# Squared-ReLU MLP on one core: another order of terms, block sums, conversions and the tail around the Down stages

## The chip, the cores and the metric

The kernel runs on one core of a Trainium2 chip. The metric is device time in microseconds (us), the median of three runs. The engines are TensorE (PE in the profile, its weight loads PEld), VectorE (DVE), ScalarE (ACT), GpSimd (POOL) and SyncE (SP), which issues most of the DMA transfers. Each engine executes its own instructions in order; semaphores order them between engines.

## The reference

A decoder trunk of two layers on 512 tokens of width 1024, in float32. Layer A mixes tokens by a short gated convolution, layer B by native sparse attention; both then add a squared-ReLU MLP. The change touches only the MLPs and the final norm:

```python
def rms_norm(x, g):
    xf = x.astype(jnp.float32)
    y = xf * lax.rsqrt(jnp.mean(xf * xf, axis=-1, keepdims=True) + EPS)
    return (y * g.astype(jnp.float32)).astype(x.dtype)

def squared_relu_mlp(h, w1, w2):
    return jnp.square(jax.nn.relu(h @ w1)) @ w2        # w1 1024 x 4096, w2 4096 x 1024
...
        x = x + squared_relu_mlp(rms_norm(x, norm_mlp[layer]), mlp_w1[layer], mlp_w2[layer])
...
    return rms_norm(x, final_norm)
```

## The kernel before

**Numbers.** Every matrix product runs in fp16: each float32 operand is split into a high half (hi) and the rest (lo), and three matmuls make a term: hi·hi, hi·lo and lo·hi. The residual stream `X` stays in SBUF, features on the partitions, as 8 tiles of 128 x 512 tokens. The RMS norm's factor per token is not put on the MLP's input but on the result of the first product.

**Weights.** They come in *pieces* in the order in which they are used. A piece is loaded by SP into one of three staging slots (`wst`, L157 for the MLP's second matrix), then split: ACT writes the hi half (L184, L195), DVE the lo half (L185, L196). `ahead()` (L215) converts until AHEAD2 = 3 pieces of the second matrix (AHEAD = 2 of others) lie in front of the one in use; when a piece's conversion is through, the load of a later one into its slot is issued.

**MLP.** Each layer's MLP is done in two halves of 2048 hidden features. For each half `mlp_up` runs 8 pairs of hidden tiles, 48 matmuls of 512 columns a pair on PE (`mm3`, L341 to L343). Then for each pair (`mlp_up`, L499 to L505): DVE multiplies relu by the row factor `rb` (`ml_t`), ACT squares (`ml_z`, L501), POOL makes four sums of 256 columns (`R_SUMS`, L503), ACT writes the hi half `rh` (L504) and DVE the lo half `rl` (L505). The factor `rb` is made once in a layer, in the first pair: a matmul sums the squares, `rstd_of` (L295) takes ACT's square root (L298) and refines its inverse in five small DVE steps (L300 to L305; the last, L305, writes `rs_r`), PE spreads the row over the partitions (L312), ACT scales it (L317).

`mlp_down` multiplies by the second matrix with seven products in place of eight, by Winograd's scheme for 2 x 2 blocks: the four blocks of the weights give seven operands by four sums on DVE (`W_SUMS`, L182, in place in the staging slot, before the split), the hidden side has its seven from `R_SUMS`. There are 4 pairs of output tiles; a pair takes 8 chunks of the hidden features, a chunk 7 products of 3 matmuls (L550 hi·hi, L551 weight hi by relu lo, L552 weight lo by relu hi), 256 columns each. Chunk c reads what `mlp_up` wrote in its pair c, so the last chunk reads the last `rl`. A piece holds two chunks of weights, so a pair takes four pieces. The seven products are summed over the chunks in PSUM halves: pairs 0 and 2 in two banks `a` and two `b`, pairs 1 and 3 in two `c`, a `d` and an `e`. 

`combine` puts the seven results together into `X`: an ACT copy of P1 (`dn_p`, L520), then DVE steps (L517 with a scalar, L527, L531, L533). It is a generator, `post`: one step of it is issued after each chunk of the next pair, with the conversions of `ahead()` in between.

**The tokens' form of the result.** In the last of the four Down stages, `mid_b` is called after chunk 5 of a pair: `token_major` (L1168) has PE transpose the pair before into tokens on the partitions, in banks `a` or `c`. ACT squares (L1162) and copies (L1177, to `xsh` and `xsl` under the program's tile names) and POOL multiplies by the gains (L1178). The last pair is done by `last_b` (L1205): its first half as chunks, then its seven products one after the other, each with its combine steps behind it; the last transposes (L1166); and `store` (L1187) for two token tiles at a time: the sum of squares, the inverse root, the scaling (ACT half of the columns, L1195; DVE the others, L1198 to L1202) and the store on SP's queue (L1203).

**What sets the order.** The program is written in one order, and a scheduler moves instructions on each engine; `tc.issue_after(ins)` adds one edge, so that what is issued in its scope stands behind `ins` on that engine.

Of the kernel before, what the change touches and what calls it, by code (L numbers as in the profile page):

```python
# [48 lines left out]
def body(ctx, tc, x, rel_bias, norm_mix, norm_mlp, mlp_w1, mlp_w2, a_w_in, a_conv_w, a_w_out,  # L49
         kv_norm, w_kv, cmp_pe_k, cmp_pe_v, phi_k_w1, phi_k_w2, phi_v_w1, phi_v_w2,  # L50
         b_w_qg, b_w_o, final_norm, ident_c, onehot_c, out):
    nc = tc.nc
# [118 lines left out]
    def convert_piece(step=1024):  # L171
# [7 lines left out]
        if shape is None:  # L179
            b = t.rearrange("p (k b n) -> p k b n", k=2, n=128)  # L180
            for e, o, x, y in W_SUMS:
                DVE.tensor_tensor(b[:, :, o], b[:, :, x], b[:, :, y], op=e)  # L182
# [110 lines left out]

    def rstd_of(ss):
# [10 lines left out]
        DVE.scalar_tensor_tensor(r, t, 1.5, r, op0=OP.add, op1=OP.mult)  # L305
# [201 lines left out]

    def combine(p, acc7, done):
# [11 lines left out]
        ACT.activation(p1, P1, AF.Copy, scale=sc)  # L520
# [17 lines left out]
    def mlp_down(rh, done, mid=None, last=None):  # L538

        post = iter(())  # L540
        for p in range(4):
# [3 lines left out]
            def product(i, c, w):  # L545
                a, b = PRODUCTS[i]
                wh, wl = (u[:, a - 1] for u in w)
                xh, xl = (u[:, c, b - 1] for u in rh)
                other = i % 2 == 1
                PE.matmul(acc7[i], wh, xh, start=c == 0 and not other, stop=False, skip_group_check=other)  # L550
                PE.matmul(acc7[i], wh, xl, start=False, stop=False, skip_group_check=other)  # L551
                PE.matmul(acc7[i], wl, xh, start=False, stop=c == 7, skip_group_check=other)  # L552
# [20 lines left out]
            post = combine(p, acc7, done)  # L573
        drain(post)
# [570 lines left out]
    with pool("hidden_b") as hp:  # L1145
# [22 lines left out]
        def token_major(p, h, tag):  # L1168
# [4 lines left out]
            for i in range(2):  # L1173
# [3 lines left out]
                ACT.activation(o, v, AF.Copy)  # L1177
                POOL.tensor_tensor(o, o, gains(p), op=OP.mult)  # L1178

        def mid_b(p):  # L1180
            if p:
                for h in range(2):
                    token_major(p - 1, h, "a" if p % 2 else "c")
# [4 lines left out]
        def store(h, late=None):  # L1188
            sst = work.tile([128, 2], F32, name="sst", bufs=2)
            DVE.tensor_reduce(sst, ssf[:, 2 * h:2 * h + 2], axis=mybir.AxisListType.X, op=OP.add)  # L1190
            r = rstd_of(sst)
            for i in range(2):
                t = 2 * h + i
                a, b = xt[t][:, 0:512], xt[t][:, 512:1024]
                ACT.activation(a, a, AF.Copy, scale=r[:, i:i + 1])  # L1195
                if late:
                    b = xt[t][:, 512:768]
                    DVE.scalar_tensor_tensor(xt[t][:, 768:896], late[i], r[:, i:i + 1], gains(3, 1),  # L1198
# [85 lines left out]
```

## Time and profile before

| | us |
|---|---|
| median of three runs | 1137.95 (1136.97 to 1138.77) |
| profiled execution | 1136.88 |
| its span | 1135.1 |
| busy: PE | 1095.8 (97%) |
| busy: DVE | 832.3 (73%) |
| busy: ACT | 568.5 (50%) |
| busy: POOL | 157.6 (14%) |

The profile is one execution; its time stands beside its span, which begins with the first instruction. In the rows below a line begins with the start in us and the duration, then the engine, the line of the kernel, the operation, the tile written and those read, and in brackets the idle time ahead of it on its engine with what ended it. Rows that begin with two numbers and a colon are stretches of the span: the length, then the busy time of PE (count), PEld, DVE, ACT, POOL and SP, the granted TensorE clock, the DMA share and GB/s. A row of several instructions has "xcount", and the duration from the first start to the last end or their sum.

Each layer has up, Down, up, Down. The four Down stages begin at 266.4, 424.4, 882.5 and 1040.7 in the span; between the second and the third lie the shared K/V side, the attention and the first up stage of layer B.

### The profile page before, as it was taken

The numbers are of one execution on the slowest core, as the hardware profiler recorded it, in microseconds if no ns is written. First come the engines' busy times: TensorE is split into PE (matmuls) and PEld (weight loads), VectorE is DVE, ScalarE is ACT, GpSimd is POOL, SyncE is SP. The second block draws the span as 40 slices with busy tenths as digits, with TensorE's granted clock in tenths as the row PEclk, the third lists the DMA queues.
The fourth block names the chain that finished last, engine by engine and source line by source line (L and its number), as shares of the span: only waits on it lengthen the run. The fifth ranks groups of instructions, "written<-read, shape, count | busy, mean of one in ns | idle before, by whom it ended". The sixth has DMA issues, their size and how long they took to land.

```text
span 1135.1 us, 20099 instructions
## 1 busy us (share of the span) xinstructions
PE 1095.8 (97%) x7959; PEld 694.1 (61%) x7959; DVE 832.3 (73%) x1498; ACT 568.5 (50%) x922; POOL 157.6 (14%) x198
## 2 busy tenths in 40 slices
PE   8999999999999999999999989899999999999985
PEld 4444444446884448865767666664444787445874
DVE  4755458765897556999589969896895598754795
ACT  4532235444433444556679777765544433343452
POOL 0000000422000221001002022220122100123020
PEclk9999999999999999999999999999999999999998
DMA  6433335333333333313334341112633333330221
GB/s 210 130 94 97 107 105 172 113 93 113 112 112 112 111 95 107 112 42 120 112 78 122 83 138 38 39 38 74 187 111 112 111 109 115 105 95 7 84 84 75
DMA packets 149378, 115.75 MB, mean 102 GB/s; under 512 B 8612, under 2 KB 146564, under 8 KB 149284
## 3 DMA queue, kind: packets, MB, share of 16 engines
q1 hardware_dynamic: 146736, 109.47, 31.8%
q10 hardware_dynamic: 2260, 4.40, 1.3%
q8 instruction: 62, 1.02, 0.4%
q0 software_dynamic: 288, 0.61, 0.2%
q14 instruction: 32, 0.26, 0.1%
HBM read 110.22 MB, written 2.14 MB: 99 GB/s over the span
## 4 chain that ended last, share of the span: by engine, by line
PE 50%; DVE 19%; ACT 11%; issue 7%; POOL 7%; DMA 5%; SPq 1%; DVEq 0%; ACTq 0%; POOLq 0%
POOL ml_z L503 6%; PE a L341 4%; PE a L342 4%; PE a L343 4%; DVE wlo L185 4%; DMA wst<-mlp_w_dram 3%; ACT rh L504 3%; PE c L343 3%; PE c L342 3%; PE c L341 3%; PE b L342 3%; PE b L341 3%; PE b L343 3%; DVE wlo L196 3%; DVE ml_t L499 2%
## 5 line engine op out<-in xcount | busy, mean ns | idle before, releaser
L195 ACT ACTIVATE whi<-wst 128x1024 f16<-128x1024 f32 (+4 forms) x171 | 142.4, 858 | 127.9 <-PE b L342 38.4
L196 DVE SCALAR_TENSOR_TENSOR wlo<-wst,whi 128x1024 f16<-128x1024 f32 (+4 forms) x171 | 169.9, 1001 | 40.2 <-ACT whi L195 39.9
L503 POOL TENSOR_TENSOR ml_z<-ml_z 128x256 f32<-128x256 f32 x128 | 99.9, 801 | 610.1 <-ACT ml_z L501 410.1
L184 ACT ACTIVATE whi<-wst 128x1792 f16<-128x1792 f32 x64 | 106.9, 1692 | 135.4 <-DVE wst L182 102.3
L341 PEld LDWEIGHTS <-whi 128*128 128x128 f16 x1024 | 100.4, 98 | 112.3 <-issue 5.5
L343 PEld LDWEIGHTS <-wlo 128*128 128x128 f16 x1024 | 100.2, 98 | 112.1 <-issue 0.4
L342 PEld LDWEIGHTS <-whi 128*128 128x128 f16 x1024 | 100.2, 98 | 107.6 <-issue 2.0
L505 DVE TENSOR_TENSOR rl<-ml_z,rh 128x1792 f16<-128x1792 f32 x32 | 64.8, 2026 | 135.9 <-ACT rh L504 135.7
L185 DVE SCALAR_TENSOR_TENSOR wlo<-wst,whi 128x1792 f16<-128x1792 f32 x64 | 128.8, 2019 | 3.0 <-ACT whi L184 2.9
L182 DVE TENSOR_TENSOR wst<-wst 128x256 f32<-128x256 f32 x256 | 108.9, 469 | 24.4 <-DMA wst<-mlp_w_dram 23.4
L504 ACT ACTIVATE rh<-ml_z 128x1792 f16<-128x1792 f32 x32 | 54.3, 1698 | 106.1 <-POOL ml_z L503 106.1
L551 PEld LDWEIGHTS <-whi 128*128 128x128 f16 x896 | 87.7, 98 | 16.2 <-issue 5.6
L552 PEld LDWEIGHTS <-wlo 128*128 128x128 f16 x896 | 87.6, 98 | 15.0 <-issue 4.2
L550 PEld LDWEIGHTS <-whi 128*128 128x128 f16 x896 | 87.7, 98 | 10.5
L343 PE MATMUL b<-xsh,wlo 128*128 128x512 f16 x208 | 78.8, 379 | 0.0
L342 PE MATMUL b<-xsl,whi 128*128 128x512 f16 x208 | 78.8, 379 | 0.0
L341 PE MATMUL b<-xsh,whi 128*128 128x512 f16 x208 | 78.7, 379 | 0.0
L501 ACT ACTIVATE ml_z<-ml_t 128x1024 f32<-128x1024 f32 x32 | 33.8, 1057 | 88.4 <-DVE ml_t L499 88.4
L963 ACT ACTIVATE at_p<-at_s,at_m 128x128 f32<-128x128 f32 (+3 forms) x128 | 71.0, 557 | 13.7 <-DVE at_m L961 12.6
L551 PE MATMUL a<-rl,whi 128*128 128x256 f16 x256 | 69.8, 273 | 3.7 <-DVE rl L505 3.7
L341 PE MATMUL c<-xsh,whi 128*128 128x512 f16 x192 | 72.8, 379 | 0.0
L342 PE MATMUL c<-xsl,whi 128*128 128x512 f16 x192 | 72.8, 379 | 0.0
(309 smaller groups left out, 2686.4 us busy)
## 6 DMA issues: line engine op xcount, KB each, us to landing
wst<-mlp_w_dram SPq DMA_DIRECT2D x256, 256.0 KB, 3.3
wst<-a_w_in_dram SPq DMA_DIRECT2D x18, 512.0 KB, 3.5
wst<-w_kv_dram SPq DMA_DIRECT2D x12, 512.0 KB, 3.5
T<-ext_d ACTq DMA_DIRECT2D x4, 1056.0 KB, 6.0
wst<-a_w_out_dram SPq DMA_DIRECT2D x8, 512.0 KB, 3.4
wst<-b_w_qg_dram SPq DMA_DIRECT2D x8, 512.0 KB, 3.5
wst<-b_w_o_dram SPq DMA_DIRECT2D x8, 512.0 KB, 3.3
wst<-a_w_in_dram SPq DMA_DIRECT2D x8, 384.0 KB, 5.5
```

The costliest lines, as they stand in the source:

```text
L182: DVE.tensor_tensor(b[:, :, o], b[:, :, x], b[:, :, y], op=e)
L184: ACT.activation(hi, b[:, :, 1:], AF.Copy, scale=sc)
L185: DVE.scalar_tensor_tensor(lo, b[:, :, 1:], sc, hi, op0=OP.mult, op1=OP.subtract)
L195: ACT.activation(hi[:, s:e], w, AF.Copy, scale=sc)
L196: DVE.scalar_tensor_tensor(lo[:, s:e], w, sc, hi[:, s:e], op0=OP.mult, op1=OP.subtract)
L341: PE.matmul(ps, w[0], xs[0], start=start, stop=False)
L342: PE.matmul(ps, w[0], xs[1], start=False, stop=False)
L343: PE.matmul(ps, w[1], xs[0], start=False, stop=stop)
L503: POOL.tensor_tensor(z[:, o], z[:, a], z[:, b], op=e)
L504: ACT.activation(rh[0][:, p], z[:, 1:8], AF.Copy)
L550: PE.matmul(acc7[i], wh, xh, start=c == 0 and not other, stop=False, skip_group_check=other)
L551: PE.matmul(acc7[i], wh, xl, start=False, stop=False, skip_group_check=other)
```

## The change

It has four parts.

1. *Order of terms.* In every product of `mlp_down` the weight's lo half is now taken second and relu's lo half third. In the first pair's last chunk all seven products take their first two terms first, and then all seven the third.
2. *Block sums.* `W_SUMS` of a piece are issued behind the last step of the inverse root that was built last (`root_op`). And `combine`'s first step (P6, P7) is issued as soon as it exists, ahead of the next pair's conversions.
3. *Conversions behind the copies.* In the first chunk of each later pair the conversions are issued behind the ACT copy `dn_p` of the pair before. In the last stage those of chunk 4 move to after chunk 5, behind the last ACT copy of the tokens.
4. *Tail.* The last pair's products run in the order P1, P6, P5, P7, P3, P2, P4. The first two token tiles are scaled by DVE alone, all columns, behind the sum of P4; for the other two ACT scales the lower half of the columns and stores it on its own queue, DVE the upper, stored on SP's.

```diff
@@ convert_piece
-            for e, o, x, y in W_SUMS:
-                DVE.tensor_tensor(b[:, :, o], b[:, :, x], b[:, :, y], op=e)
+            with tc.issue_after(root_op[0].ins):
+                for e, o, x, y in W_SUMS:
+                    DVE.tensor_tensor(b[:, :, o], b[:, :, x], b[:, :, y], op=e)
@@ rstd_of
-        DVE.scalar_tensor_tensor(r, t, 1.5, r, op0=OP.add, op1=OP.mult)
+        root_op[0] = DVE.scalar_tensor_tensor(r, t, 1.5, r, op0=OP.add, op1=OP.mult)
@@ combine
-        ACT.activation(p1, P1, AF.Copy, scale=sc)
+        copied[0] = ACT.activation(p1, P1, AF.Copy, scale=sc)
@@ mlp_down
-            def product(i, c, w):
+            def product(i, c, w, terms=(0, 1, 2)):
...
-                PE.matmul(acc7[i], wh, xh, start=c == 0 and not other, stop=False, skip_group_check=other)
-                PE.matmul(acc7[i], wh, xl, start=False, stop=False, skip_group_check=other)
-                PE.matmul(acc7[i], wl, xh, start=False, stop=c == 7, skip_group_check=other)
+                for n in terms:
+                    PE.matmul(acc7[i], wl if n == 1 else wh, xl if n == 2 else xh, stop=c == 7 and n == 2,
+                              start=c == 0 and n == 0 and not other, skip_group_check=other)
...
-                    for i in range(7):
-                        product(i, c + k, [u[:, k] for u in w])
-                    if c + k == 5 and mid:
-                        mid(p)
-                    if k == 0:
-                        drain(ahead())
-                    next(post, None)
+                    for terms in ((0, 1), (2,)) if p == 0 and c + k == 7 else ((0, 1, 2),):
+                        for i in range(7):
+                            product(i, c + k, [u[:, k] for u in w], terms)
+                    behind = None
+                    if c + k == 0 and p:
+                        behind = copied[0]
+                    if c + k == 5 and mid and p:
+                        behind = mid(p)
+                    if k == (1 if c == 4 and mid else 0):
+                        with tc.issue_after(behind.ins) if behind else nullcontext():
+                            drain(ahead())
+                    if c + k or not p:
+                        next(post, None)
...
             post = combine(p, acc7, done)
+            next(post)
@@ last_b
             product(2)
             stt(wv[:, 1], P6, p1)
             DVE.tensor_tensor(X1[:, n1], X1[:, n1], p1, op=OP.add)
+            product(4)
+            stt(both, P5[:, None, :].to_broadcast([128, 2, 256]), both)
             product(3)
             stt(wv[:, 0], P7, wv[:, 1])
             DVE.tensor_tensor(both, both, wv, op=OP.add)
-            product(4)
-            stt(both, P5[:, None, :].to_broadcast([128, 2, 256]), both)
...
-                DVE.tensor_tensor(xt[t][:, 768:1024], ps[:, 0:256], gains(3), op=OP.mult)
-            store(0)
+                early.append(ps[:, 0:256])
+            r = root(0)
...
-                DVE.tensor_tensor(xt[t][:, 896:1024], ps[:, 0:128], gains(3)[:, 128:256], op=OP.mult)
+                early.append(ps[:, 0:128])
             product(6)
-            stt(X2[:, n1], P4, X2[:, n1])
+            final = DVE.scalar_tensor_tensor(X2[:, n1], P4, sc, X2[:, n1], op0=OP.mult, op1=OP.add)
...
-            store(1, late)
+            with tc.issue_after(final.ins):
+                for t in range(2):
+                    DVE.scalar_tensor_tensor(xt[t][:, 768:1024], early[t], r[:, t:t + 1], gains(3),
+                                             op0=OP.mult, op1=OP.mult)
+                    DVE.tensor_scalar(xt[t][:, 0:768], xt[t][:, 0:768], r[:, t:t + 1], None, op0=OP.mult)
+                    put(t, nc.sync)
+            r = root(1)
+            for i in range(2):
+                t, c = 2 + i, r[:, i:i + 1]
+                ACT.activation(xt[t][:, lo], xt[t][:, lo], AF.Copy, scale=c)
+                put(t, nc.scalar, lo)
+                DVE.scalar_tensor_tensor(xt[t][:, 768:896], late[i], c, gains(3, 1), op0=OP.mult, op1=OP.mult)
+                DVE.scalar_tensor_tensor(xt[t][:, 896:1024], early[t], c, gains(3)[:, 128:256],
+                                         op0=OP.mult, op1=OP.mult)
+                DVE.tensor_scalar(xt[t][:, 512:768], xt[t][:, 512:768], c, None, op0=OP.mult)
+                put(t, nc.sync, hi)
```

`root(h)` makes the sum of squares and the inverse root as `store` did; `put(t, queue, at)` issues the store of one token tile's columns on a queue. The number of matmuls stays.

More of the change, by code (lines that the diff above doesn't have):

```diff
@@ L1 @@
 import math
-from contextlib import ExitStack
+from contextlib import nullcontext, ExitStack
 import numpy as np
@@ L292, in split_gain @@
         return hi
+    root_op = [None]
     def rstd_of(ss):
@@ L1176, in token_major, with root, put @@
                 square(v, t, p)
[L1177 removed]
+                last = ACT.activation(o, v, AF.Copy)
                 POOL.tensor_tensor(o, o, gains(p), op=OP.mult)
+            return last
         def mid_b(p):
[L1181 to L1183 removed]
+            return [token_major(p - 1, h, "a" if p % 2 else "c") for h in range(2)][1]
         def done_b(p):
             yield
[L1188 removed]
+        def root(h):
             sst = work.tile([128, 2], F32, name="sst", bufs=2)
             DVE.tensor_reduce(sst, ssf[:, 2 * h:2 * h + 2], axis=mybir.AxisListType.X, op=OP.add)
[L1191 to L1198, printed above, removed]
[L1199 to L1203 removed]
+            return rstd_of(sst)
+        def put(t, queue, at=slice(0, D)):
+            queue.dma_start(out[0, t * 128:(t + 1) * 128, at], xt[t][:, at])
         def last_b(acc7, product):
@@ L1232, in last_b @@
             stt(X1[:, n1], P2, X1[:, n1])
+            lo, hi = slice(0, 512), slice(512, 1024)
+            early = []
             for t in range(2):
```

6 lines of the change are left out of this document (1 added, 5 removed).

## The prediction

> **What bounds the kernel now.** The page first: its span, and the shares of the chain that ended last.
>
> ```profile
> span 1135.1 us, 20099 instructions
> PE 50%; DVE 19%; ACT 11%; issue 7%; POOL 7%; DMA 5%; SPq 1%; DVEq 0%; ACTq 0%; POOLq 0%
> ```
>
> Half of the chain is PE, so elsewhere other engines hold PE up. Where, is read from busy time by stretch (first Down stage, and the last with the tail; PE's busy time stands behind the length):
>
> ```profile
> 266.41:341.45 75.04, 73.46 (x673) 65.69 (x672) 60.48 (x93) 31.16 (x23) 5.64 (x8) 1.00 0.37 113
> 1040.60:1135.10 94.50, 78.67 (x706) 69.00 (x703) 65.09 (x112) 38.64 (x74) 14.88 (x20) 0.96 0.22 73
> ```
>
> A Down stage is 672 matmuls. The first loses under 2 us; the last stretch has 15.8 us without PE. PE's timeline shows each wait (in brackets the idle time and who ended it):
>
> ```profile
> 193.86 0.29 PE L312 MATMUL e<-ident,rs_r 128*128 128x128 f32 x1 [0.90 <-DVE rs_r L305]
> 284.31 0.27 PE L551 MATMUL a<-rl,whi 128*128 128x256 f16 x1 [1.58 <-DVE rl L505]
> 286.70 0.27 PE L552 MATMUL c<-rh,wlo 128*128 128x256 f16 x1
> 441.00 0.27 PE L551 MATMUL a<-rl,whi 128*128 128x256 f16 x1 [0.30 <-DVE rl L505]
> 809.48 0.32 PE L312 MATMUL e<-ident,rs_r 128*128 128x128 f32 x1 [0.92 <-DVE rs_r L305]
> 900.62 0.27 PE L551 MATMUL a<-rl,whi 128*128 128x256 f16 x1 [1.79 <-DVE rl L505]
> 1080.87 0.27 PE L550 MATMUL a<-rh,whi 128*128 128x256 f16 x1 [2.46 <-ACT xsh L1177]
> 1082.15 0.27 PE L550 MATMUL a<-rh,whi 128*128 128x256 f16 x1 [0.47 <-ACT xsl L1177]
> 1101.30 0.27 PE L550 MATMUL c<-rh,whi 128*128 128x256 f16 x1 [0.43 <-ACT xsh L1177]
> 1102.58 0.27 PE L550 MATMUL c<-rh,whi 128*128 128x256 f16 x1 [0.46 <-ACT xsl L1177]
> 1111.84 0.30 PE L1166 MATMUL a<-ident,X 128*128 128x128 f32 x1 [0.59 <-DVE X L531]
> 1116.84 0.27 PE L550 MATMUL c<-rh,whi 128*128 128x256 f16 x1 [0.77 <-DVE dn_w L1213]
> 1121.80 0.38 PE L1166 MATMUL a<-ident,X 128*128 128x128 f32 x2
> ```
>
> The inverse root: 0.90 + 0.92 = 1.82. Relu's lo in the last chunk: 1.58 + 0.30 + 1.79 = 3.67 (none in the last Down stage). PSUM banks that ACT reads late: 2.46 + 0.47 + 0.43 + 0.46 = 3.82. The last pair: 0.59 + 0.77 = 1.36. In all 10.7 us, and the edits name each of them. A matmul takes 0.109 (73.46 over 673).
>
> **Lo last.** Relu's lo was asked for by the chunk's 2nd matmul and will be by its 15th: 13 x 0.109 = 1.42 us later, nearly the whole wait. But what is late next is on the same engine:
>
> ```profile
> 282.23 2.03 DVE L505 TENSOR_TENSOR rl<-ml_z,rh 128x1792 f16<-128x1792 f32 x1 [4.70 <-ACT rh L504]
> 284.17 2.02 DVE L185 SCALAR_TENSOR_TENSOR wlo<-wst,whi 128x1792 f16<-128x1792 f32 x1
> ```
>
> Behind rl stands the weights' lo half of the second pair's first piece, ending 286.19. The pair needed it third in a product (286.70); now it is taken second, at 286.59. The room is 0.40, less some 0.04 between an end and the start that it releases: 0.36. So the edit is worth 0.36 where rl binds, at most 0.30 in the second stage, and 0 in the last: the wait moves from rl to wlo. In the changed order wlo still follows rl.
>
> **Block sums behind the root.** In layer B the sums wait for a load, with the root behind them:
>
> ```profile
> 804.75 0.26 ACT L298 ACTIVATE rs_r<-d,eps 128x4 f32<-128x4 f32 x1
> 806.89 1.10 DVE L182 TENSOR_TENSOR wst<-wst 128x256 f32<-128x256 f32 x3 [2.19 <-DMA wst<-mlp_w_dram]
> 809.26 0.16 DVE L305 SCALAR_TENSOR_TENSOR rs_r<-rs_t,rs_r 128x4 f32<-128x4 f32 x1
> ```
>
> Freed, its four later steps, 0.2 apart, end at 805.9; in layer A at 189.8 (square root at 188.8, as ACT no longer converts a piece ahead of it). Both PE waits go. That does not move Down by itself: what it waits for is the relu chain, ml_t, square, four POOL sums, hi, lo, weights' lo, then ml_t of the next pair. Its last two rounds end with the rl at 272.03 and at 282.23 (10.20 apart), while PE needs some 10.4 a pair (48 matmuls of twice these columns): the chain runs behind PE and keeps the lag that it gets in the first three pairs. There:
>
> ```profile
> 201.19 5.64 POOL L503 TENSOR_TENSOR ml_z<-ml_z 128x256 f32<-128x256 f32 x4 [197.56 <-DMA wst<-mlp_w_dram]
> 212.99 5.08 POOL L503 TENSOR_TENSOR ml_z<-ml_z 128x256 f32<-128x256 f32 x4 [6.16 <-ACT ml_z L501]
> 226.03 3.47 POOL L503 TENSOR_TENSOR ml_z<-ml_z 128x256 f32<-128x256 f32 x4 [7.96 <-ACT ml_z L501]
> 272.03 2.03 DVE L505 TENSOR_TENSOR rl<-ml_z,rh 128x1792 f16<-128x1792 f32 x1 [4.70 <-ACT rh L504]
> 231.27 2.03 DVE L505 TENSOR_TENSOR rl<-ml_z,rh 128x1792 f16<-128x1792 f32 x1 [1.02 <-ACT rh L504]
> 847.59 2.03 DVE L505 TENSOR_TENSOR rl<-ml_z,rh 128x1792 f16<-128x1792 f32 x1
> ```
>
> POOL's four sums take 5.64, 5.08 and 3.47, because DVE's conversions and block sums run beside them. I put the changed order on each engine in time with these rows' durations (hi 1.70, lo 2.02, a block sum 0.34 alone and 0.95 when it takes turns with POOL). Layer A: ml_t ends 196.7, rl of the first pair at 207.8, of the second at 219.5, of the third at 232.0 against 233.30: 1.3 earlier. In the second pair nine block sums now stand in one train; if POOL gets no turn in it, the third rl comes 0.9 later instead. Layer B: 849.1 against 849.62, 0.5 earlier, or 1 later without turns. I take turns, as the 3.47 shows them. The first Down stage gains 1.3 + 0.36 = 1.66 (bounds -0.5 and the 2.5 of both its waits), the third 0.5 + 0.36 = 0.86 (-0.6 and 2.7).
>
> The Trainium skill ("SBUF — State Buffer", Who interferes with whom) says that of a VectorE instruction with two SBUF inputs and a GpSimd one that reads SBUF the second to issue blocks until the first has ended. By it turns are right, and longer trains cost POOL one block sum for each of its four; the rows agree with blocking, and the sum would be the same.
>
> **Pairs summed at once.** The sums of a pair come before its successor's conversions instead of among them: no instruction more. In the second Down stage, and in the last up to the third pair's end, DVE has little room (its busy time is the third number behind the length):
>
> ```profile
> 447.00:505.60 58.60, 58.19 (x501) 48.52 (x498) 56.36 (x99) 26.54 (x31) 0.00 (x0) 1.00 0.24 75
> 1081.40:1111.70 30.30, 28.49 (x257) 24.93 (x255) 29.18 (x44) 12.30 (x23) 5.33 (x7) 1.00 0.22 70
> ```
>
> With 56.36 us of work in 58.60 and PE busy all but 0.41, another order gains nothing in the second stage: I take 0, with bounds of -0.6 (the time of one hi half's wait, by which lo halves shift) and of 0.3, that stage's wait on rl. On SP one load of an up piece moves ahead of a Down piece's in the first stages, and a piece's load is issued when its slot's lo half ends, so a lo half put back puts its load back too; the three slots hold loads well ahead of PE, so this costs only where a load is already the releaser, in the last stage.
>
> **The last Down stage.** Its pairs take four pieces each; I number pieces 1 to 16. ACT converted 10 and 11 ahead of the tokens' copies; that is what held the banks:
>
> ```profile
> 1076.26 3.29 ACT L184 ACTIVATE whi<-wst 128x1792 f16<-128x1792 f32 x2 [3.18 <-DVE wst L182]
> 1077.99 2.02 DVE L185 SCALAR_TENSOR_TENSOR wlo<-wst,whi 128x1792 f16<-128x1792 f32 x1 [0.42 <-ACT whi L184]
> 1081.43 2.71 DVE L182 TENSOR_TENSOR wst<-wst 128x256 f32<-128x256 f32 x4 [1.41 <-DMA wst<-mlp_w_dram]
> 1075.79 0.88 SPq L157 DMA_DIRECT2D wst<-mlp_w_dram  x2
> 1100.72 3.57 DVE L182 TENSOR_TENSOR wst<-wst 128x256 f32<-128x256 f32 x4 [0.60 <-DMA wst<-mlp_w_dram]
> 1111.02 0.68 DVE L531 TENSOR_TENSOR X<-X,dn_w 128x512 f32<-128x512 f32 x1
> ```
>
> Now the copies come first, free the banks by 1076.0, and PE opens the third pair at 1078.3 (1080.87 less its wait). But the changed order on DVE puts piece 12's block sums ahead of the lo halves of 10 and 11 (1077.99 was 10's). 12's load is issued when 9's lo ends (1075.79; the slot is 9's) and lands near 1080.0, at worst 1081.4. Sums 1.4, 10's lo 1.95: 1083.3. PE asks for it at its 44th matmul, 1082.9: a wait of 0.4, at worst 1.8. From there DVE has no pause: pieces 11 and 12, the second pair's sums (done 1092.3, as PE turns them at 1092.4), 13, block sums of 14 and 15 in turns with POOL to 1099.0; then 16's load, issued at 13's end (1094.6) and 4.4 us on its way like the one before 1100.72; its sums 1.4, three lo halves 5.8, the rest of the third pair 3.5: 1109.8. Before, that was 1111.70, and PE's last transposes followed at 1111.84. So of 3.82 us at the banks and 0.59 here 1.9 stay; the rest goes into DVE's queue. Bounds 0.5 and 4.4.
>
> **The tail.** Products now run P1, P6, P5, P7: while DVE sums P6 (what 0.77 waited for), PE has P5. The 72 matmuls before the next transposes fill 7.85; before, 1111.84 + 0.90 to 1121.80 was 9.06: 1.2 gained. After them:
>
> ```profile
> 1125.97 0.88 DVE L1202 TENSOR_SCALAR xsh<-xsh,rs_r 128x512 f32<-128x512 f32 x2
> 1127.76 0.16 DVE L1190 TENSOR_REDUCE sst<-ssf 128x2 f32<-128x10 f32 x1 [0.91 <-ACT ml_t L1162]
> 1129.13 1.33 ACT L1195 ACTIVATE xsl<-xsl,rs_r 128x512 f32<-128x512 f32 x2 [0.88 <-DVE rs_r L305]
> 1129.95 1.05 SPq L1203 DMA_DIRECT2D out_dram<-xsl  x2
> ```
>
> The second root began 5.96 behind the transposes, kept back by ACT's scaling of the first tokens. Now DVE scales these alone, ahead of the second reduce. The first scaling stood 4.17 behind the transposes; two multiplications by the gains ahead of it are gone (I take 0.9, three of the small DVE steps here), so 3.3. Scaling: 1.5 times 0.88 for 768 columns of two token tiles and 0.6 for their other 256: 1.9. That makes 5.2. The root takes 1.37 as before (1127.76 to 1129.13); then ACT scales two halves (1.33) and issues two stores on its own queue (1.05 by SP's row): 9.0 to the last issue's end, 9.2 before. 0.2 gained; bounds -0.6, if DVE's columns cost as much as ACT's, and 1.2, if stores go out while ACT scales. The last stage in all: 1.9 + 1.2 + 0.2 = 3.3.
>
> **The sum.** 1.66 + 0 + 0.86 + 3.3 = 5.8. The profiled execution took 1136.88, so 1131.1; the median of the runs lies 1.07 above it, and that gives 1132.1.
>
> **Rivals.** First, *every named wait goes in full*: 10.7, and 0.3 of the tail's stores: 1126.9. For it, PE's waits are short and each has an edit; against it, the two orders above, where DVE's next conversion is the next wait. Second, *DVE is the bound*: piece 12's load lands at 1081.4 as before, the third pair's X ends at 1111.7 as before, and the relu chains end no earlier, but for 0.36 in each layer: 0.36 + 0.36 + 1.2 + 0.2 = 2.1: 1135.8. For it, 29.18 us of DVE's work in 30.30; against it, the 1.41 of idle at 1081.43, which the new order fills. Third, the other side: *trains of block sums starve POOL*. In the second and third up pair of each layer the four POOL sums wait out nine block sums in a row (9 x 0.34 = 3.1), then take 2.9 alone: 6.0 in place of 5.08 and 3.47, so 3.4 later, less the 0.9 by which the root lets the chain start earlier: 2.5 in each layer. Less 0.36 each, 4.3 are lost against 3.3 gained in the last stage: 1139.0. It decides from the point where the chains come 2.0 later in each layer. For it the 5.64 at 201.19; against it the 3.47 at 226.03, with block sums running beside.
>
> **How the numbers follow.** Forecast 0.55, every wait in full 0.15, DVE the bound 0.18, starved POOL 0.08, others 0.04 (not what the edits say, either sign). A measurement here tells about 0.2%, 2.3 us, from no change. Faster: 0.52 of the forecast's 0.55, the first rival's 0.15, half of the second's (0.09): 0.76. Slower: most of the third and half of the others: 0.07. Same: the other 0.17. The terms' bounds together give -1.7 to 11.5; they won't all fall on one side, and with a tenth left out at either end gains run from 1.9 to 9.4: 1136.0 to 1128.5.
>
> **What would show it.** Right: the waits on rs_r gone; PE waiting for wlo at the second pair's start, 0.8 in the first Down stage (0.90 + 1.58 - 1.66) and 1.1 in the third, and in the last chunk for rl not at all in layer A and 0.8 in layer B (0.92 + 1.79 - 0.5 - 1.42; with the 1.1 it makes 2.71 - 0.86); none of PE's waits on ACT's copies; 0.4 for wlo two chunks into the last stage's third pair; the last pair's first transposes 31.7 behind the third pair's start (31.0 before, 1080.87 to 1111.84); stores ending on ACT's queue. Wrong: a wait on rl of over 1.5 us; POOL's four sums over 5 us in the second up pair; piece 16's block sums ending more than 25 us behind the third pair's start, where I have 22.2.

## The result, and the profile after

| | before | changed |
|---|---|---|
| median of six runs, us | 1137.54 (1136.97 to 1138.77) | 1133.13 (1130.68 to 1134.19) |
| ratio, 95% interval | | 0.9957 (0.9945 to 0.997) |
| profiled execution, its span | 1136.88, 1135.1 | 1133.21, 1131.2 |

The kernel is faster by 4.4 us in the medians (4.8 in the means, on which the ratio rests; 3.4 to 6.3 by the interval). The prediction had 1132.1 and a range from 1128.5 to 1136.0, so the time lies inside it, 1.0 above the forecast. But its terms did not come out one by one as they were worked out: two were too small, one did not show, and a stretch that the change does not touch lost 1.2 us in the first profile.

The changed kernel's page: its span and the shares of the chain that ended last.

```profile
span 1131.2 us, 20054 instructions
PE 43%; DVE 23%; ACT 11%; POOL 9%; issue 8%; DMA 5%; SPq 1%; DVEq 0%; ACTq 0%; POOLq 0%
```

PE's share of the chain fell from 50% to 43% and VectorE's (DVE) rose from 19% to 23%: the end hangs on VectorE's queue more than before. Busy time by stretch, the four Down stages of the changed kernel (PE's stands behind the length, the granted clock third from the end):

```profile
265.31:340.00 74.69, 73.68 (x673) 65.66 (x672) 61.32 (x96) 31.11 (x23) 5.62 (x8) 1.00 0.37 113
422.89:496.25 73.36, 73.36 (x673) 65.69 (x672) 61.81 (x96) 34.59 (x35) 4.06 (x6) 1.00 0.28 86
881.21:957.17 75.96, 73.83 (x673) 65.64 (x672) 61.50 (x95) 31.31 (x23) 5.63 (x8) 1.00 0.37 112
1040.00:1131.20 91.20, 78.06 (x706) 68.87 (x703) 62.94 (x110) 37.47 (x71) 19.23 (x20) 0.97 0.23 76
```

In the second stage PE is busy all of 73.36 us, where before it lost about 1. The third still loses 2.1, the last 13.1 (15.8 before). PE's timeline gives the waits that are left:

```profile
285.09 0.28 PE L557 MATMUL c<-rh,wlo 128*128 128x256 f16 x1 [0.91 <-DVE wlo L186]
850.55 0.39 PE L346 MATMUL a<-xsh,wlo 128*128 128x512 f16 x1 [0.94 <-DVE wlo L197]
898.27 0.27 PE L557 MATMUL a<-rh,whi 128*128 128x256 f16 x1 [0.85 <-ACT rh L507]
900.33 0.60 PE L557 MATMUL a<-rl,whi 128*128 128x256 f16 x4 [0.37 <-DVE rl L508]
902.27 0.28 PE L557 MATMUL c<-rh,wlo 128*128 128x256 f16 x1 [0.91 <-DVE wlo L186]
1083.63 0.28 PE L557 MATMUL a<-rh,wlo 128*128 128x256 f16 x1 [1.15 <-DVE wlo L186]
1109.89 1.09 PE L1179 MATMUL a<-ident,X 128*128 128x128 f32 x8 [2.40 <-DVE X L536]
```

The waits on the inverse root and on ScalarE's copies are gone. In their place stand waits for the weights' lo half at the second pair's start (0.91, in both layers), for relu's hi half (0.85), for a lo half two chunks into the third pair (1.15) and for X (2.40).

The gain along the span, from the starts of the same matmuls in the two profiles: 1.10 at the first Down stage's start (266.41 to 265.31), 1.50 at its end, 2.46 at the second's end (498.60 to 496.14), only 1.25 where layer B's up stage starts (797.22 to 795.97), 0.63 at the third Down stage's end, 1.95 at the last transposes (1111.84 to 1109.89), 3.9 at the span's end. The 1.2 between 496 and 796 lie in the attention, which the change does not touch. One stretch of the changed kernel, and of the kernel before the stretch of the same work:

```profile
715.90:719.50 3.60, 3.60 (x43) 3.44 (x42) 2.28 (x11) 2.55 (x8) 0.00 (x0) 0.56 0.01 2
```

```profile
718.20:721.00 2.80, 2.46 (x44) 2.12 (x43) 2.28 (x11) 2.50 (x9) 0.00 (x0) 1.00 0.00 0
```

The granted clock was 0.56 for 3.6 us here and 1.00 there: the same matmuls took 3.6 us in place of about 2.4. The kernel before has a stretch at half clock too, but it ends at 718.09, just ahead of this work, after 3.41 us; the changed kernel's lasts 6.83, from 712.22 to 719.05. Such stretches differ between executions of one kernel (in its second profile the changed kernel has 3.41 us there), so a profile's sum can be off by 1 us for this alone.

### The profile page after: what moved, and what is told of

Same layout as the page of the kernel before. It is cut to its first block, busy times and chain, and to the rows that moved or that the text cites. A ratio compares the mean times of both kernels' runs of the same rounds, so it can differ in the third digit from the quotient of the medians.

```text
span 1131.2 us, 20054 instructions
## 1 busy us (share of the span) xinstructions
PE 1097.7 (97%) x7959; PEld 696.8 (62%) x7959; DVE 829.6 (73%) x1496; ACT 567.0 (50%) x920; POOL 161.2 (14%) x198
## 3 DMA queue, kind: packets, MB, share of 16 engines
q8 instruction: 62, 1.02, 0.4%
## 4 chain that ended last, share of the span: by engine, by line
PE 43%; DVE 23%; ACT 11%; POOL 9%; issue 8%; DMA 5%; SPq 1%; DVEq 0%; ACTq 0%; POOLq 0%
POOL ml_z L506 8%; DVE wlo L186 6%; ACT rh L507 4%; PE a L344 4%; PE a L345 4%; PE a L346 4%; DMA wst<-mlp_w_dram 4%; DVE wst L183 3%; PE b L345 3%; PE b L346 3%; PE b L344 3%; DVE ml_t L502 3%; DVE wlo L197 3%; ACT ml_z L504 3%; PE c L345 2%
## 5 line engine op out<-in xcount | busy, mean ns | idle before, releaser
L183 DVE TENSOR_TENSOR wst<-wst 128x256 f32<-128x256 f32 x256 | 103.6, 455 | 24.5 <-DMA wst<-mlp_w_dram 23.4
L346 PE MATMUL c<-xsh,wlo 128*128 128x512 f16 x192 | 72.8, 379 | 0.0
L557 PE MATMUL c<-rh,wlo 128*128 128x256 f16 x256 | 69.8, 273 | 1.8 <-DVE wlo L186 1.8
```

Of the source, the lines that this page charges most:

```text
L346: PE.matmul(ps, w[1], xs[0], start=False, stop=stop)
L557: PE.matmul(acc7[i], wl if n == 1 else wh, xl if n == 2 else xh, stop=c == 7 and n == 2, start=c == 0 and n == 0 and not other, skip_group ...
```

## Experiments

All readings in one table. The three lengths are those of the first three Down stages, from the first matmul's start to the last one's; "to turns" runs from the last stage's first matmul to the last pair's first transposes, "to end" to the span's end. The ratio is to the kernel before, in runs on the same chip.

| kernel | ratio (95%) | first | second | third | to turns | to end |
|---|---|---|---|---|---|---|
| before | | 74.99 | 74.21 | 75.22 | 71.15 | 94.40 |
| changed | 0.9957 (0.9945, 0.997) | 74.60 | 73.25 | 75.87 | 69.83 | 91.15 |
| changed, again | 0.9957 (0.9945, 0.997) | 74.58 | 73.28 | 75.84 | 68.60 | 89.93 |
| lo last alone | 0.9984 (0.9975, 0.9992) | 74.62 | 73.25 | 74.92 | 71.08 | 94.38 |
| order of terms alone | 0.9974 (0.9963, 0.9986) | 74.83 | 73.25 | 75.16 | 70.10 | 93.33 |
| split of the last chunk alone | 0.9995 (0.9983, 1.0006) | 74.46 | 74.96 | 74.80 | 71.06 | 94.31 |
| sums behind the root alone | 0.9999 (0.999, 1.0009) | 74.91 | 74.23 | 77.42 | 70.86 | 94.13 |
| pairs summed at once alone | 1.0004 (0.9995, 1.0012) | 74.91 | 74.11 | 75.24 | 71.30 | 94.56 |
| copies first alone | 1.0015 (1.0005, 1.0026) | 74.91 | 73.95 | 75.00 | 70.75 | 93.96 |
| copies first alone, again | 0.9998 (0.9987, 1.0008) | 74.91 | 73.85 | 75.27 | 70.38 | 94.48 |
| copies first, with an order edge | 0.9959 (0.9945, 0.9974) | 74.93 | 74.00 | 75.25 | 66.44 | 89.79 |
| tail alone | 0.9987 (0.9978, 0.9995) | 74.94 | 74.08 | 75.23 | 71.04 | 92.24 |
| changed without copies first | 0.9944 (0.9931, 0.9956) | 74.56 | 73.66 | 75.87 | 69.67 | 90.91 |
| changed, with the order edge | 0.9923 (0.9911, 0.9935) | 74.58 | 73.47 | 75.85 | 66.77 | 88.65 |

### One part at a time

**Lo last alone**: the new `product` and the split last chunk, on the kernel before.

```diff
-                    for i in range(7):
-                        product(i, c + k, [u[:, k] for u in w])
+                    for terms in ((0, 1), (2,)) if p == 0 and c + k == 7 else ((0, 1, 2),):
+                        for i in range(7):
+                            product(i, c + k, [u[:, k] for u in w], terms)
```

> Only the order of terms is changed, and the first pair's last chunk. My theory: the wait moves from relu's lo to the weights' lo half behind it on VectorE. The two stages that wait over 1 us for relu's lo (1.58 and 1.79) keep a wait 0.36 shorter, shown at a weight's lo half at the second pair's start (1.2 and 1.4); the second stage loses its 0.30: 1.0 us less in all. Rival, the waits go in full: 3.7 less. Rival, the order of terms also removes the second stage's two waits of 0.2 to 0.3 on weights' lo halves at 489.47 and 494.33: then that stage is 73.25 long as in the changed kernel (74.21 before).

The first stage is 0.37 shorter, the third 0.30: the wait moved to the lo half, as expected (0.90 us at 286.19 in its trace). The second is 0.96 shorter, with no wait left, which the theory did not have and the second rival did. Where that comes from is settled below.

**Sums behind the root alone**: `with tc.issue_after(root_op[0].ins):` around `W_SUMS`.

> Only the block sums stand behind the inverse root. My theory: both waits on rs_r (0.90, 0.92) go, and in layer A the relu chain ends 1.2 earlier (rl of the first half's last pair at 283.1 against 284.26), so the first Down stage ends 1.2 us earlier; in layer B the chain hangs on VectorE's whole queue and on the loads, and ends within 0.3 of before: the wait on relu's lo grows there by what PE comes earlier, 0.9. In all 1.2 to 1.5 less. Rival, the waits saved stay saved: 1.8. Rival, the chain does not move in either layer: 0, with both waits on relu's lo 0.9 longer.

In layer A it does what it should: the first Down stage starts at 264.75 (before 266.41) and ends 1.74 earlier. But in the runs nothing is left. In layer B, PE reaches the last chunk earlier than its data, and its timeline and stretches of busy time show what follows:

```profile
896.67 0.27 PE L553 MATMUL a<-rh,whi 128*128 128x256 f16 x1 [0.40 <-ACT rh L507]
898.73 0.27 PE L554 MATMUL a<-rl,whi 128*128 128x256 f16 x1 [1.79 <-DVE rl L508]
```

```profile
899.30:903.00 3.70, 3.70 (x21) 2.70 (x19) 3.25 (x2) 2.35 (x3) 0.00 (x0) 0.54 0.20 60
903.00:957.60 54.60, 54.60 (x503) 48.93 (x502) 47.06 (x83) 18.88 (x13) 0.00 (x0) 1.00 0.36 113
```

After two waits of 0.40 and 1.79 us the granted clock was 0.54 over these 3.7 us, of which 3.41 are at 0.50: 16 matmuls began 0.213 apart in place of 0.109, 1.7 us more. (The count of 21 in the row includes matmuls that began ahead of it.) Third stage 77.42, which is 2.2 longer than before: the 0.40, the 1.7 and 0.1 more. So my theory held in layer A, and in layer B the saved wait came back as a longer one with a price on top. One execution was profiled, so how often the clock falls here is not shown.

**Pairs summed at once alone**: `next(post)` behind `combine`, and the first chunk's conversions behind `dn_p`.

> Only the first step of combine is issued at once, and the conversions of a pair's first chunk behind its ScalarE copy. My theory by the prediction: nothing in the first three stages (second stage 74.2 as before), and in the last stage nothing by itself, as ScalarE's conversions still stand ahead of the tokens' copies: 0. Rival: the 0.96 us that the second stage lost in the changed kernel is this part's: the second stage is 73.3 to 73.7 long (0.30 of its waits was on relu's lo and may stay).

Second stage 74.11, ratio 1.0004: nothing, as forecast. The rival falls.

**Copies first alone**: the conversions of chunk 4 in the last stage behind the tokens' copies.

> Only the conversions of chunk 4 in the last stage are put behind the tokens' copies. My theory: PE's four waits on the copies (2.46, 0.47, 0.43, 0.46) go, and most of it comes back as a wait for weights' lo halves in the third pair (1.3 in the changed kernel) and on X ahead of the last transposes (2.4 there, 0.59 before): last transposes 0.7 to 1.4 us earlier, and that is the gain. Rival, the waits go in full: 3.8. Rival, VectorE is the bound from 1081 on: the last transposes at 1111.8 as before, 0.

The last transposes come 0.4 earlier, below my 0.7 to 1.4, and the runs took 0.15% more. PE's wait at the banks is gone, but VectorE's and PE's timelines show what it turned into:

```profile
1080.54 1.56 DVE L182 TENSOR_TENSOR wst<-wst 128x256 f32<-128x256 f32 x4 [3.22 <-DMA wst<-mlp_w_dram]
1082.01 2.02 DVE L185 SCALAR_TENSOR_TENSOR wlo<-wst,whi 128x1792 f16<-128x1792 f32 x1
```

```profile
1084.09 0.28 PE L552 MATMUL a<-rh,wlo 128*128 128x256 f16 x1 [1.55 <-DVE wlo L185]
```

VectorE stood 3.22 us at piece 12's block sums, for their load, with the lo half of piece 10 behind them, for which PE waited 1.55. Of the three theories "VectorE is the bound" comes nearest.

**Tail alone**: `root`, `put` and the new `last_b`.

> Only the tail is changed. My theory, by the prediction: from the last pair's first transposes to the next ones 1.2 us less (before 9.95, in the changed kernel 8.95), and 0.2 less from there to the end; by the changed kernel's profile the second part is worth 0.9 (13.30 before, 12.37). In all 1.4 to 1.9 us less. Rival: the new tail only works when the third pair's X comes late; alone it gives less than 0.7.

From the last pair's first transposes to the next ones 8.92 (before 9.95), from there to the end 12.28 (13.30): 1.03 and 1.02, 2.05 in all in the profile, 1.5 in the runs (0.6 to 2.5). The rival falls.

By their ratios the parts alone come to 1.3 or 3.2 us in sum (with the first or the second runs of copies first), against 4.9 for all four together. Each ratio is uncertain by about 1 us, so whether the parts help one another can't be told from the sums.

### What repeats

**The changed kernel again.**

> The changed kernel once more, to see which of its readings repeat. The first block sums of layer B began 11.31 us behind the up stage's first matmul (9.67 to 10.22 in four other kernels), because their load landed late. If that is chance, it is 9.7 to 10.2 here, the third Down stage ends 1.0 to 1.6 us earlier against the up stage's start (161.11 there), and the time is 1131 to 1132. If the order of loads causes it, it is above 11 again and the time 1133. The third pair's wait for a weight's lo half (1.31) and the wait for X before the last transposes (2.4) come from the order on VectorE and repeat within 0.3.

Its median is 1132.77. Layer B's first block sums began 9.90 us behind the up stage's first matmul: the 11.31 was chance. In this profile the third Down stage ends 160.26 behind that matmul (161.11 in the first, 160.49 before). Over all fourteen profiles the block sums begin between 9.67 and 11.31 behind it; the profile of before, on which the prediction rests, is the earliest. The wait for X repeats (2.4), the third pair's wait for a lo half does not: its load landed earlier, VectorE stood 2.10 us for it (2.77 in the first profile), and PE did not wait. The 1.15 that it waited in the first profile is nearly all of the difference between 69.83 and 68.60.

**Copies first again.**

> Conversions behind the tokens' copies alone, once more, to catch a slow run in a profile (1137.5 or more, two of three). If my theory holds, VectorE's block sums of the third pair's fourth-last piece begin later than 40.6 us behind the last stage's start, because the load lands later, PE waits over 2.5 us for the lo half and over 3.5 for X, and the granted clock is as before. By the rival the loads land as they did, and the time is lost at a lower granted clock behind a wait of PE, or outside the last stage.

The profiled run took long (span 1136.3, against 1134.0), and neither theory had it whole. PE's waits are those of the first look (1.2 for the lo half, 1.55 there; 2.93 for X, as there), so no later load. Behind the second wait stands this stretch:

```profile
1112.21 1.76 PE L1168 MATMUL a<-ident,X 128*128 128x128 f32 x8 [2.93 <-DVE X L531]
```

```profile
1113.70:1116.00 2.30, 2.30 (x14) 1.64 (x12) 0.00 (x0) 2.17 (x10) 1.97 (x3) 0.54 0.00 0
```

Again a granted clock near half behind a wait; from these transposes to the next ones it took 10.82 us, where the first profile has 9.95, so 0.9 was lost there, near the end, where nothing hid it. That was the rival's mark. But of the 2.3 us between the two spans 1.8 lie ahead of the last stage, where this part changes nothing. Why the median of this kernel was 0.15% above the one before in the first runs and level in the second stays open.

### What freed the second stage

**Order of terms alone**: every product takes the weight's lo half second; the last chunk is not split.

> Only the order of the three terms, without the split of the last chunk. The scheduler then puts combine's steps ahead of the next piece's first block sum in the first Down stage, as in the kernel with both. My theory: that order, not the split, is what freed the second stage: VectorE no longer waits 0.63 and 0.65 there for a load with combine behind it, relu's lo of the next half ends 1.4 to 1.8 us earlier (369.55 before), the second stage is 73.3 long (74.21), and the first keeps its wait on relu's lo (1.5 to 1.7, stage 75.0). Rival: the split does it, and the second stage is 74.1.

**Split alone**: the old order in all products, the first pair's last chunk in two passes.

```diff
+            def product(i, c, w, terms=(0, 2, 1)):
...
+                    for terms in ((0, 1), (2,)) if p == 0 and c + k == 7 else ((0, 2, 1),):
```

> Only the split of the first pair's last chunk (its first pass takes weight hi by relu hi and weight hi by relu lo's partner, the weight's lo half by relu hi, its second relu's lo), all other products in the old order of terms. My theory: the first stage gains what the wait on relu's lo leaves to the weight's lo half, which is then asked for one matmul later than in the changed kernel: 0.36 to 0.5 (stage 74.5 to 74.65), the second its 0.30 (73.8 to 73.95), the third 0.3 to 0.5. Rival, that it frees the second stage by itself: 73.3.

The theory holds: order of terms 73.25, split 74.96, even longer than before. VectorE's timeline ahead of a combine in the first Down stage, first before, then with the order of terms alone:

```profile
327.35 2.02 DVE L185 SCALAR_TENSOR_TENSOR wlo<-wst,whi 128x1792 f16<-128x1792 f32 x1
330.02 0.42 DVE L182 TENSOR_TENSOR wst<-wst 128x256 f32<-128x256 f32 x1 [0.65 <-DMA wst<-mlp_w_dram]
330.36 0.42 DVE L517 SCALAR_TENSOR_TENSOR X<-a,X 128x256 f32<-128x256 f32 x1
```

```profile
327.19 2.02 DVE L185 SCALAR_TENSOR_TENSOR wlo<-wst,whi 128x1792 f16<-128x1792 f32 x1
329.12 0.42 DVE L517 SCALAR_TENSOR_TENSOR X<-a,X 128x256 f32<-128x256 f32 x1
```

Before, one block sum stood ahead of the combine and waited 0.65 for a load (0.63 in the pair before it). With the new order of terms the scheduler put it behind. VectorE fills the load's time with the combine, and relu's first lo half of the next up stage ends at 368.33 in place of 369.55; in the kernel with both edits at 367.77. That lead is kept for eight pairs and takes away all of the second stage's waits. With the split alone the block sum stays in front (0.66 at 330.64), and the second stage waits four times for lo halves (from start to start 0.25 to 0.54 us more than 0.109). The new order moved some ten such block sums in the four Down stages, and no run moves one of them alone: that the order of terms frees the stage is shown, that it does so through these rows is read from the traces. In two later kernels with the same order small waits remain (stages of 73.66 and 73.47).

### The order edge

**Changed kernel without copies first**: chunk 4's conversions stay where they were.

> The changed kernel, but the last stage's conversions of chunk 4 are issued where they were, ahead of the tokens' copies. By the profiles the part is worth 1.3 us (last transposes 71.15 behind the stage's start before, 69.83 changed), so this is 1.3 slower than the changed kernel: 1134.4. Rival, from the runs of that part alone, which took 1.7 us more than before in the median: its long wait for X ahead of the last transposes costs TensorE's clock in many runs, and without the part the kernel is 1 to 2 us faster: 1131.5.

1131.18, not the 1134.4 of my theory: within the changed kernel, too, this part is worth nothing that could be told (its interval and the changed kernel's overlap). The last transposes stand between the two readings of the changed kernel. The rival had the time; its reason, the clock, does not show in this profile and stays open.

**Changed kernel with the order edge**: in the last three pairs of the last stage a piece's block sums stand behind the lo half of the piece two before (`los` collects the lo halves' instructions).

```diff
-            with tc.issue_after(root_op[0].ins):
+            with tc.issue_after((los[-2] if i >= len(pieces) - 12 else root_op[0]).ins):
                 for e, o, x, y in W_SUMS:
...
-            DVE.scalar_tensor_tensor(lo, b[:, :, 1:], sc, hi, op0=OP.mult, op1=OP.subtract)
+            los.append(DVE.scalar_tensor_tensor(lo, b[:, :, 1:], sc, hi, op0=OP.mult, op1=OP.subtract))
```

> The changed kernel, with one order edge in the last three pairs of the last stage: a piece's block sums stand behind the lo half of the piece two before. In the changed kernel VectorE idles 2.6 us at 1077.4 and 1.5 at 1097.5 for a load, with lo halves waiting behind the block sums. My theory (that order is the term of the prediction that was paid): the wait for a lo half in the third pair (1.31) goes, and X ahead of the last transposes (2.4) is waited for less than 0.7: last transposes 2.5 to 3.7 us earlier, 1129.5 to 1130.5. Rival, VectorE is the bound whatever the order: the lo halves come earlier but X as late as now, so PE waits 3.7 for X: 0.

1128.92 (1127.57 to 1129.04), ratio 0.9923: faster than both kernels by any reading here. VectorE's timeline in the third pair, in the changed kernel and with the edge:

```profile
1080.08 1.56 DVE L183 TENSOR_TENSOR wst<-wst 128x256 f32<-128x256 f32 x4 [2.77 <-DMA wst<-mlp_w_dram]
1081.56 3.95 DVE L186 SCALAR_TENSOR_TENSOR wlo<-wst,whi 128x1792 f16<-128x1792 f32 x2
1098.96 1.88 DVE L183 TENSOR_TENSOR wst<-wst 128x256 f32<-128x256 f32 x4 [1.49 <-DMA wst<-mlp_w_dram]
```

```profile
1075.40 3.96 DVE L186 SCALAR_TENSOR_TENSOR wlo<-wst,whi 128x1792 f16<-128x1792 f32 x2 [3.17 <-ACT whi L185]
1079.28 0.42 DVE L522 SCALAR_TENSOR_TENSOR dn_w<-c,dn_p 128x256 f32<-128x256 f32 x1
1079.62 0.41 DVE L183 TENSOR_TENSOR wst<-wst 128x256 f32<-128x256 f32 x1
```

The two lo halves run while the load is on its way. The edge also moved the block sums of piece 7, from 976.15, where they stood ahead of the last up stage's relu chain and waited 1.74 for a load, to 1052.93. So VectorE enters the last stage with a lead of 3.0 us (its last rl starts 10.7 behind the stage's start, 13.7 without the edge). It gives this lead back at 1075.40, where it waits 3.17 for ScalarE's hi half; that is ready 37 us behind the stage's start in both kernels. From there on the order in the third and fourth pair differs: the load of piece 12, for which the changed kernel stands until 40.0 behind the stage's start, is not asked for before 41.2. PE has no wait in the third pair and 0.67 for X; the last transposes come 66.77 behind the stage's start, 3.1 and 1.8 earlier than in the two profiles of the changed kernel. The rival (VectorE the bound whatever its order) falls.

**Copies first with the same edge**, on the kernel before.

> Conversions behind the tokens' copies alone, with the order edge (block sums of the last three pairs' pieces behind the lo half of the piece two before). My theory: that part alone lost time because VectorE stood at block sums whose load was late while lo halves waited behind them; with the edge the third pair's wait for a lo half (1.71 in its profile) and most of the wait for X (3.2 less 0.3) go: last transposes 67 to 68.5 us behind the stage's start (70.75 there), 1134 to 1135.5 us, and no run above 1137.5. Rival: its slow runs (8 of 12 between 1137.5 and 1140.8) come from TensorE's clock or from another stage: the last stage gets shorter in the profile, but the median stays at 1137 or more.

Last transposes at 66.44, 4.3 and 3.9 earlier than without the edge; 1133.18, ratio 0.9959, no run above 1135.58. So with that order on VectorE this part no longer loses what it gains. The edge without this part was not run, so how the 4.8 us (1137.97 to 1133.18) divide between the two stays open.

## Why the prediction was right, and where not

- **Lo last**, 0.36 in the first and third stage: 0.37 and 0.30 in the kernel with that part alone. The mechanism held: the wait moves to the lo half behind it (0.91 at 285.09, forecast 0.8).
- **Layer A's relu chain**, 1.3 earlier: relu's last lo half ends 1.15 earlier (284.25 to 283.10), and 1.74 earlier with that part alone. The rival of starved POOL falls: the sums of the second pair took 3.48 us (5.08 before), those of the third 3.48, as the turns in the forecast had it (its row stands below, with one from layer B where POOL had no turn). First stage in all: 1.50 and 1.87 in two profiles for 1.66.
- **The second stage**, forecast 0 with an upper bound of 0.3: 0.96. The step "With 56.36 us of work in 58.60 ... another order gains nothing" failed. A full queue is no proof that order is worth nothing, because the lag it carries was made a stage earlier, where VectorE stood 0.63 and 0.65 at a load. The forecast gave the moved block sums no price.
- **Layer B**, forecast 0.86: the third stage ended 0.62 later against the up stage's start in the first profile and 0.23 earlier in the second. The wait on the root went (in its place 0.94 at 850.55 in the first). The chain there hangs on its first load, as the prediction quoted for the block sums, but I took the landing time of one profile as fixed. From the first block sum to the third pair's relu lo it takes 42.73 us before and 42.07 and 42.67 after; the landing itself moves by up to 1.6. In the two other kernels with this chain it is 42.03 and 42.37, so counted from the landing the 0.5 of the forecast is about right (0.1 to 0.7), and what the term left out is the landing itself. Of the waits that it forecast in the third stage, 0.8 for rl and 1.1 for the lo half, came 0.37 and 0.91, and one of 0.85 for relu's hi half, which it did not have.
- **The third pair of the last stage**, forecast 1.9 with 0.5 to 4.4: 1.32 and 2.55 in two profiles. The wait for a lo half, forecast 0.4 and at worst 1.8, was 1.15 and 0; X was forecast to be ready 69.1 behind the stage's start (1109.8 less 1040.69) and came at 69.8 and 68.6. The step that named piece 12's block sums ahead of two lo halves was right, and the order edge shows its price: 1.8 to 3.1 us. That the mean of the two profiles is the forecast's 1.9 is luck all the same. The term comes from taking PE's waits at the banks away, and the changed kernel without copies first, which keeps them (1.99 and 0.46), has its last transposes at 69.67, 1.48 earlier than before: the other parts bring this gain, by a way that no run isolates, and copies first adds nothing to it that could be told.
- **The tail**, 1.2 and 0.2: 1.00 and 0.93. The second term was mis-sized. The forecast let the scalings and the two stores on ScalarE's queue follow one another (1.33 and 1.05). The trace has the first store's issue at 1125.88, while the second half is being scaled (1125.12 to 1126.46), and the second reduce 4.9 behind the transposes for 5.2. The upper bound of that term, 1.2, named this case. ScalarE's rows in the changed kernel:

```profile
1125.12 1.34 ACT L1266 ACTIVATE xsl<-xsl,rs_r 128x512 f32<-128x512 f32 x2 [0.88 <-DVE rs_r L308]
1125.88 0.98 ACTq L1206 DMA_DIRECT2D out_dram<-xsl  x2
```

In sum the terms were 1.7, 0, 0.9, 1.9, 1.4 (5.8), and showed, in the mean of the two profiles, 1.7, 1.0, -0.2, 1.9, 1.9 (6.3): the second stage and the tail made up for layer B. The attention took back 1.2 and 0.2, and the two executions gained 3.7 and 7.1 (1136.88 to 1133.21 and to 1129.79; the second is the fastest of its six runs), with the medians' 4.4 between them. A slip in the forecast's working: the bounds that it gives for its terms add up to gains from -0.6 to 12.3 (with the 1.2 of the last pair as it stands), not from -1.7 to 11.5; its range lies inside both.

The granted clock was no term of the prediction, and it should have been one. The Trainium skill ("TensorE: Matmul & The Clock Gate", What's actually happening) has the clock fall to half after an idle window of about 3.4 us. The traces agree on the half (0.50 from 899.47 to 902.88 in the kernel with the sums behind the root) but not on the wait: there 0.40 and 1.79 us, with one matmul between them, were enough. What decided it is shown in the last section.

## What to carry to other kernels

An in-order engine that stands at a load loses whatever could have run behind it. Before a change of order is costed, look for rows that wait for a DMA while a ready conversion or combine stands behind them; here an order edge at such places was worth 3.9 us (1132.77 to 1128.92), nearly as much as the whole change.

A scheduler's order is part of the change. An edit on one engine (the order of three matmuls) moved block sums on another, and the stage that this freed (0.96) gained more than those at which the edit aimed (0.37 and 0.30).

A sum of terms under 1 us each rests on one profile's landing times and clock. Take a second profile before a term is read from a wait for a DMA.

## What the runs showed of the hardware

- A wait of TensorE can cost a second time, and where it falls decides it. In every profile the stretches at half clock ahead of the tail last 3.41 or 6.83 us and begin whole multiples of 3.41 us apart. With each span outside the attention cut into intervals at these points, half clock follows each of the 40 intervals in which PE idled for 2.03 us or more, and none of some 3270 in which it idled for 1.99 or less. (In the attention it also followed intervals with 0.6 to 2.0 us of idle time, so idle time alone is not the whole rule.) In the last stage of the eight kernels without copies first, PE waited 2.0 to 2.6 us for the same PSUM bank. In five at least 2.1 us of idle time lay in one interval, and 11 to 15 matmuls behind it began 0.213 apart in place of 0.109, 1.1 to 1.6 us more; in the other three no interval has more than 1.99. In the kernel before, the wait of 2.46 was cut in two by such a point. Busy time in the two intervals, with the order of terms alone and before (PE's behind the length, the clock third from the end):

```profile
1077.31:1080.72 3.41, 1.30 (x13) 1.02 (x11) 3.29 (x4) 3.41 (x11) 1.12 (x2) 1.00 0.36 118
1080.73:1084.13 3.40, 3.11 (x16) 2.06 (x15) 3.37 (x4) 2.55 (x6) 2.33 (x3) 0.50 0.46 149
```

```profile
1076.49:1079.89 3.40, 1.92 (x18) 1.56 (x17) 2.94 (x4) 3.40 (x5) 0.00 (x0) 1.00 0.51 158
1079.90:1083.31 3.41, 1.97 (x17) 1.62 (x17) 2.00 (x4) 2.48 (x12) 3.05 (x4) 1.00 0.46 147
```

  The loss was hidden there, as the transposes waited for VectorE's X: they come 70.1 to 71.3 behind the stage's start in seven of the eight, with and without it.
- A load's landing scatters. Layer B's first loads are a burst, and in the first profile of the changed kernel SP issued all of them 1.25 us earlier than before, at the same distances up to the one that by its place releases the first block sums (800.45 against 801.70); yet these began 0.39 later (807.28 against 806.89).
- VectorE's block sums and POOL's sums take turns: beside each other a block sum took 0.95 and a POOL sum 0.90, alone 0.42 and 0.72. Beside a train of conversions POOL had no turn: the first of its four sums took 4.35 us, while two lo halves of 2.02 and one of 1.22 ran, and the four together 6.52, where they take 2.89 alone. The second pair of layer A and the first of layer B in the changed kernel:

```profile
212.22 3.48 POOL L506 TENSOR_TENSOR ml_z<-ml_z 128x256 f32<-128x256 f32 x4 [8.09 <-ACT ml_z L504]
814.10 6.52 POOL L506 TENSOR_TENSOR ml_z<-ml_z 128x256 f32<-128x256 f32 x4 [39.19 <-ACT ml_z L504]
```
